# First block of a two-block transformer on one core: weights-moving products 512 wide, the residual's affine on VectorE, and the gated mix's affine taken through the token mix

## The chip, the cores and the metric

The kernel runs on one core of a Trainium2 chip. The metric is the device time of one execution in microseconds, and it is the median of three executions where a table says so. The engines are TensorE (PE, with its weight loads shown apart as PEld), VectorE (DVE), ScalarE (ACT), GpSimd (POOL) and SyncE (SP), which issues the DMA transfers.

## The reference

There are 256 tokens of 1024 features. The first block has two layers; layer 0 mixes with an RWKV-7 part and a differential attention (`ab_w_in`, `ab_w_out`), layer 1 with a gated token mix (`c_w_in`, `c_w_out`). The second block, not touched by the change, takes the result.

```python
for i in range(DEPTH):                       # DEPTH = 2
    if i % 2 == 0:
        p = x @ ab_w_in[j]
        mix = concatenate([rwkv7_mix(p[..., :1792]), diff_attention(p[..., 1792:])]) @ ab_w_out[j]
    else:
        mix = chunked_spatial_gating(x, ...) @ c_w_out[j]
    x = layer_norm(DEEPNORM_ALPHA * x + mix, ln1_g[i], ln1_b[i])
    x = layer_norm(DEEPNORM_ALPHA * x + conv_ffn(x, ...), ln2_g[i], ln2_b[i])

def chunked_spatial_gating(x, w_in, b_in, ln_g, ln_b, w_s, b_s):
    u, v = split(gelu(x @ w_in + b_in), 2)                   # 1024 features each
    v = layer_norm(v, ln_g, ln_b)
    vc = v.reshape(B, S // 128, 128, 8, 128)                 # chunks of 128 tokens, 8 groups of features
    ws = w_s * tril(ones)
    mixed = einsum('gts,bcsgd->bctgd', ws, vc) + b_s.T
    return u * mixed

def conv_ffn(x, w_up, conv_w, conv_b, w_down):               # 2816 wide
    gate, val = split(x @ w_up, 2)
    return (silu(causal_conv3(gate) + conv_b) * val) @ w_down
```

## The kernel before

Every float32 weight and activation is split exactly into a high and a low part, and each product is three matmuls: high by high, high by low, low by high. `wload` fetches 128 x 1024 weights (512 KB) into `wraw` on SP's queue, ACT casts the high part `whi`, DVE subtracts to get `wlo`. There are four buffers each of `wraw`, `whi` and `wlo`, and two extra for the first weights behind a norm (`hw`).

Two forms of product exist. In `w_stat` the weights are stationary and the 256 tokens move; its result has features on partitions. In `w_mov` 128 tokens of the activations are stationary and 256 columns of weights move; its result has tokens on partitions, and the column blocks of one weight tile cover both token tiles. `nat_gemm` (the attention's q, k, v and the gate's v), `nat_out` (the output products of both mixes) and the down product inside `conv_ffn` use `w_mov`. A PSUM bank holds 512 float32 for a partition, so a bank has a column block of both token tiles. PSUM pools: `pmm` 3 banks, `pss` 2, `pst` 2, `psf` 1. `z_add` adds a finished block into the residual `z`, which has tokens on partitions (two tiles t of 128 x 1024).

`layer_norm` then runs on `z`: four `bn_stats` over 256 columns for each t, `bn_aggr`, a power on POOL for the reciprocal root (`rs`), the normalisation on DVE in two halves, eight PE transposes for each t, and for each of eight feature chunks k the gain and bias on the way out of PSUM (`xf`, `xh`, on DVE or ACT), and `xl` = `xf` - `xh` on DVE. Last it puts the gain and the bias (`lrow`) also on `z` itself, for the next residual, with four 128 x 1024 operations on POOL that are pinned in program order:

```python
pin(self.pool.tensor_tensor(v, v, rows[:, 0], ALU.mult))
pin(self.pool.tensor_tensor(v, v, rows[:, 1], ALU.add))
```

The products that come next take chunk after chunk (`w_stat_k`, three column chunks, 72 matmuls), as `xh` and `xl` arrive; between them stand steps of the second block's modulation (`fillers`, written `sf<-wraw,cs`).

`gmlp` is the gated mix: three of the u chunks in that head, then v in four column blocks, v's norm on DVE with its gain and bias on DVE for t = 0 and POOL for t = 1, meanwhile u chunks 3 to 7, and at the end the token mix: for each of 8 groups and 2 token tiles a float32 matmul of `v` by the masked `wst`, and a one-row matmul that adds the bias `bs`. A list scheduler orders the instructions of each engine by its own estimates; only pinned ones stay as written.

## Time and profile before

| what | value |
|---|---|
| time, median of 3 | 2304.64 us (2303.82 to 2312.74) |
| span of the profiled execution | 2304.2 us, mean granted clock 0.986 |
| PE busy | 2230.4 us (97%) |
| DVE / ACT / POOL busy | 1354.0 / 931.6 / 294.7 us |
| first block, about | the first 800 us |

The span goes from the first to the last instruction. The granted clock is TensorE's, 1.00 for 2.4 GHz and 0.50 for 1.2 GHz. Instructions are pipelined, so a duration overlaps the next start; a pace is the distance between starts.

### The profile page before, as it was taken

The page shows a single profiled execution, that of the slowest core. Times are in us where ns is not written, and L with a number is a line of the kernel's source. Part 1 is how long each engine was busy: PE and PEld are TensorE (multiplying, and loading weights), DVE is VectorE, ACT ScalarE, POOL GpSimd, SP SyncE. Part 2 cuts the span into 40 slices and gives each one's busy share as a digit, 9 for nine tenths or more (in the row PEclk, how much of TensorE's full clock was granted, in tenths as well). Part 3 has the DMA queues.
Part 4 walks back from the last instruction along what each step waited for, and adds up shares of the span by engine and source line. Part 5 has one row for each costly group of instructions (what it writes and reads, how often), then busy time and mean ns, then how long its engine had stood idle before and what let it go on. Part 6 is the DMA issues. An engine that isn't in the chain of part 4 may idle for free. (4 is left out here: it accounts for less than half of the span.)

```text
span 2304.2 us, 37682 instructions
## 1 busy us (share of the span) xinstructions
PE 2230.4 (97%) x15048; PEld 1936.7 (84%) x15048; DVE 1354.0 (59%) x2361; ACT 931.6 (40%) x1589; POOL 294.7 (13%) x382
## 2 busy tenths in 40 slices
PE   8999899989999999999999999999999999999999
PEld 7867799978899988657778888888889878888999
DVE  6523777674867734665566446444345566766665
ACT  5322454442445433442333334233244443345443
POOL 1153200022100002001222000000000205420000
PEclk9999999997999999999999999999999999999999
DMA  7456666573665522123442242333333233245663
GB/s 237 135 170 212 201 206 185 171 242 95 222 188 168 174 74 83 51 85 105 150 136 74 87 119 73 92 101 92 101 111 93 74 95 94 90 133 165 183 183 128
DMA packets 90640, 310.06 MB, mean 135 GB/s; under 512 B 10257, under 2 KB 12433, under 8 KB 89826
## 3 DMA queue, kind: packets, MB, share of 16 engines
q1 hardware_dynamic: 90242, 307.30, 43.1%
q8 instruction: 118, 1.93, 0.3%
q14 instruction: 56, 0.46, 0.1%
q0 software_dynamic: 224, 0.36, 0.0%
HBM read 306.58 MB, written 1.05 MB: 134 GB/s over the span
## 5 line engine op out<-in xcount | busy, mean ns | idle before, releaser
L242 DVE TENSOR_TENSOR wlo<-wraw,whi 128x1024 fp32r<-128x1024 f32 x462 | 558.0, 1211 | 391.4 <-ACT whi L321 390.4
L321 ACT CAST whi<-wraw 128x1024 fp32r<-128x1024 f32 x494 | 492.8, 1001 | 726.2 <-PE mm L276 624.4
L276 PE MATMUL mm<-hh,whi 128*128 128x256 f32 (+1 forms) x1200 | 412.9, 346 | 4.3 <-ACT hh L254 2.4
L276 PE MATMUL mm<-hh,wlo 128*128 128x256 f32 (+1 forms) x1200 | 406.3, 339 | 0.0
L276 PE MATMUL mm<-hl,whi 128*128 128x256 f32 (+1 forms) x1200 | 405.4, 338 | 0.0
L276 PE MATMUL mm<-xh,whi 128*128 128x256 f32 x880 | 252.7, 288 | 8.2 <-ACT xh L321 7.3
L276 PE MATMUL mm<-xl,whi 128*128 128x256 f32 x880 | 253.8, 288 | 3.8 <-DVE xl L242 3.7
L276 PEld LDWEIGHTS mm<-hh,whi 128*128 128x128 f32 x1200 | 227.2, 190 | 32.4 <-issue 7.9
L276 PEld LDWEIGHTS mm<-hh,wlo 128*128 128x128 f32 x1200 | 227.7, 190 | 28.8 <-issue 3.6
L276 PE MATMUL mm<-xh,wlo 128*128 128x256 f32 x880 | 251.9, 286 | 0.0
L276 PEld LDWEIGHTS mm<-hl,whi 128*128 128x128 f32 x1200 | 228.0, 190 | 25.4 <-issue 3.1
L276 PE MATMUL mm<-whi,hh 128*128 128x256 f32 x736 | 205.9, 280 | 3.2 <-ACT vn L1326 2.4
L276 PE MATMUL mm<-whi,hl 128*128 128x256 f32 x736 | 205.6, 279 | 0.0
L276 PE MATMUL mm<-wlo,hh 128*128 128x256 f32 x736 | 205.5, 279 | 0.0
L276 PEld LDWEIGHTS mm<-xh,whi 128*128 128x128 f32 x880 | 171.5, 195 | 10.8 <-ACT xh L321 7.6
L276 PEld LDWEIGHTS mm<-xl,whi 128*128 128x128 f32 x880 | 171.8, 195 | 8.7 <-DVE xl L242 6.8
L276 PE MATMUL mm<-ul,whi 128*128 128x256 f32 (+1 forms) x536 | 176.7, 330 | 0.1
L276 PE MATMUL mm<-uh,wlo 128*128 128x256 f32 (+1 forms) x536 | 176.3, 329 | 0.0
L276 PE MATMUL mm<-uh,whi 128*128 128x256 f32 (+1 forms) x536 | 176.2, 330 | 0.0
L276 PEld LDWEIGHTS mm<-xh,wlo 128*128 128x128 f32 x880 | 171.8, 195 | 0.0
L276 PEld LDWEIGHTS mm<-whi,hh 128*128 128x128 f32 x736 | 140.0, 190 | 4.2 <-ACT vn L1326 2.8
L276 PEld LDWEIGHTS mm<-whi,hl 128*128 128x128 f32 x736 | 138.2, 188 | 0.8 <-issue 0.8
(411 smaller groups left out, 3959.8 us busy)
## 6 DMA issues: line engine op xcount, KB each, us to landing
wraw<-in_w_ff SPq DMA_DIRECT2D x128, 512.0 KB, 3.7
wraw<-in_w_mod SPq DMA_DIRECT2D x96, 512.0 KB, 4.2
wraw<-in_w_up SPq DMA_DIRECT2D x88, 512.0 KB, 3.7
wraw<-in_w_gate SPq DMA_DIRECT2D x48, 512.0 KB, 3.6
wraw<-in_w_dn SPq DMA_DIRECT2D x32, 512.0 KB, 3.6
wraw<-in_w_br SPq DMA_DIRECT2D x48, 256.0 KB, 2.6
wraw<-in_w_h SPq DMA_DIRECT2D x24, 512.0 KB, 3.7
wraw<-in_w_out SPq DMA_DIRECT2D x16, 512.0 KB, 3.8
```

Of the source, the lines that this page charges most:

```text
L242: (eng or self.dve).tensor_tensor(out, a, b, ALU.subtract)
L276: self.pe.matmul(out, lhsT, rhs, start=start, stop=stop, **k)
L321: self.act.copy(hi, src)
```

## The change

1. `w_wide` moves 512 columns of weights over one token tile, so a weight tile is 2 feature chunks by 512 columns instead of 4 by 256, and a column block takes two PSUM banks, one for each t. The attention's q, k, v, both `nat_out`, the gate's v and both down products use it. In the last group of the down product, and in the late half of `nat_out`, the last column block is ordered by t.
2. `bn_stats` covers 512 columns, `z_add` one t and 512 columns.
3. The residual's gain and bias go to DVE, not pinned, written later (`do_later`).
4. In `gmlp` the gain and the bias of v's norm are no longer applied to v. The bias goes through the mix once: two matmuls of `ones` by the masked `wst` give its column sums, and eight operations make `bs` from them; the gain is a per-feature column at the way out of PSUM. The one-row bias matmuls are gone, the mask product of `wst` goes from POOL to DVE, and the mix of two groups is written behind each u chunk from 4 on. `rows3` has 1024 columns less.

```diff
+def _pack_c(w):
+    k, n = w.shape
+    return np.ascontiguousarray(
+        w.reshape(k // 256, 2, 128, n // 512, 512).transpose(3, 0, 2, 1, 4)
+    ).reshape(n // 512 * (k // 256), 128, 1024)
...
+    def w_wide(self, out, hi, lo, xh, xl, k0, t, first, last):
+
+        for k in range(2):
+            wh, wl = hi[:, k * 512:(k + 1) * 512], lo[:, k * 512:(k + 1) * 512]
+            a, b = (x[:, k0 + k, t * 128:(t + 1) * 128] for x in (xh, xl))
+            self.mm(out, a, wh, start=first and k == 0, stop=False)
+            self.mm(out, a, wl, start=False, stop=False)
+            self.mm(out, b, wh, start=False, stop=last and k == 1)
+
+    def wide_gemm(self, w, cb, xh, xl):
+
+        banks = [self.pmm(), self.pmm()]
+        for kk in range(4):
+            hi, lo = self.wload(w[cb * 4 + kk])
+            for t in range(2):
+                self.w_wide(banks[t], hi, lo, xh, xl, 2 * kk, t, kk == 0, kk == 3)
+        return banks
...
-        load = lambda cb, h: self.wload(w[cb * 2 + h])
-        banks = [self.pmm() for _ in range(3)]
-        outs = lambda b: [b[:, 0:256], b[:, 256:512]]
-        last = [self.pss(), self.pss()]
-        halves = lambda h: [(*load(3, h), 4, 4 * h)]
-        for cb in range(3):
-            self.w_mov(outs(banks[cb]), *load(cb, early), yh, yl, 4, 256, (0, 1), True, False, k0=4 * early)
-        self.last_block(z, yh, yl, halves(early), ALPHA, last, True, False)
-        tiles = [load(cb, 1 - early) for cb in range(3)]
+
+
+        banks = [[self.pmm(), self.pmm()], [self.pmm(), self.pss()]]
+        for cb in range(2):
+            for i in range(2):
+                kk = 2 * early + i
+                hi, lo = self.wload(w[cb * 4 + kk])
+                for t in range(2):
+                    self.w_wide(banks[cb][t], hi, lo, yh, yl, 2 * kk, t, i == 0, False)
+        kks = [2 - 2 * early + i for i in range(2)]
+        tiles = [[self.wload(w[cb * 4 + kk]) for kk in kks] for cb in range(2)]
         for t in range(2):
-            for cb in range(3):
-                self.w_mov([outs(banks[cb])[t]], *tiles[cb], yh, yl, 4, 256, (t,), False, t == 1, k0=4 - 4 * early)
-                if t:
-                    self.z_add(z, cb, banks[cb], ALPHA)
-        self.last_block(z, yh, yl, halves(1 - early), ALPHA, last, False, True)
-
-    def z_add(self, z, cb, ps, scale):
-        zs = z.rearrange("p (t c) -> p t c", t=2)[:, :, cb * 256:(cb + 1) * 256]
-        self.stt(zs, zs, scale, ps.rearrange("p (t c) -> p t c", t=2), ALU.mult, ALU.add)
-
-    def last_block(self, z, yh, yl, tiles, scale=1.0, banks=None, first=True, last=True):
-        """Last column block of z = scale * z + y @ w, a bank for each token tile."""
-        banks = banks or [self.pmm(), self.pmm()]
-        for i, (hi, lo, nk, k0) in enumerate(tiles):
-            for t in range(2):
-                self.w_mov([banks[t][:, 0:256]], hi, lo, yh, yl, nk, 256, (t,), first and i == 0,
-                           last and i == len(tiles) - 1, k0=k0)
-        for t in range(2 if last else 0):
-            zs = z[:, t * D + 768:t * D + 1024]
-            self.stt(zs, zs, scale, banks[t][:, 0:256], ALU.mult, ALU.add)
+            for cb in range(2):
+                for kk, (hi, lo) in zip(kks, tiles[cb]):
+                    self.w_wide(banks[cb][t], hi, lo, yh, yl, 2 * kk, t, False, kk == kks[1])
+                self.z_add(z, cb, t, banks[cb][t], ALPHA)
+
+    def z_add(self, z, cb, t, ps, scale):
+        zs = z[:, t * D + cb * 512:t * D + cb * 512 + 512]
+        self.stt(zs, zs, scale, ps, ALU.mult, ALU.add)
...
-            pin = self.tc.keep_in_program_order
-            pin(self.pool.tensor_tensor(v, v, rows[:, 0], ALU.mult))
-            pin(self.pool.tensor_tensor(v, v, rows[:, 1], ALU.add))
+            self.later.append(lambda v=v: self.mul(v, v, rows[:, 0]))
+            self.later.append(lambda v=v: self.add(v, v, rows[:, 1]))
         return xh, xl
+
+    def do_later(self, n):
+        for _ in range(min(n, len(self.later))):
+            self.later.pop(0)()
...
+                    if cp:
+                        self.do_later(2)
...
-                def down(cb, k0, nk):
-                    if c0 < 16:
-                        src = A[f"w_dn{l}"][(c0 // 8) * 8 + cb * 2 + k0 // 4]
-                    else:
-                        src = A[f"w_dt{l}"][cb][:, k0 * 256:(k0 + nk) * 256]
-                    return (*self.wload(src, nk * 256), nk, k0)
-
-                parts = [(0, 4), (4, n - 4)]
-                for cb in range(4 if c0 < 16 else 3):
-                    ps = self.pmm()
-                    for i, (k0, nk) in enumerate(parts):
-                        hi, lo = down(cb, k0, nk)[:2]
-                        self.w_mov([ps[:, 0:256], ps[:, 256:512]], hi, lo, hh, hl, nk, 256, (0, 1), i == 0, i == 1, k0=k0)
-                    self.z_add(z, cb, ps, ALPHA if c0 == 0 else 1.0)
-                if c0 == 16:
-                    self.last_block(z, hh, hl, [down(3, *q) for q in parts])
+                for cb in range(2):
+                    banks = [self.pmm(), self.pmm()]
+                    nk = n // 2
+                    tiles = [self.wload(A[f"w_dn{l}"][c0 + cb * nk + kk]) for kk in range(nk)]
+                    order = [(t, kk) for kk in range(nk) for t in range(2)]
+                    if c0 == 16 and cb:
+                        order.sort()
+                    for t, kk in order:
+                        self.w_wide(banks[t], *tiles[kk], hh, hl, 2 * kk, t, kk == 0, kk == nk - 1)
+                        if kk == nk - 1:
+                            self.z_add(z, cb, t, banks[t], ALPHA if c0 == 0 else 1.0)
...
-            self.mul(wst, wst, triu.unsqueeze(1).to_broadcast([128, 8, 128]), self.pool)
-            bs = gp.tile([1, 8, 128], F32, name="bs")
-            nc.sync.dma_start(bs, A["b_s"].rearrange("p (g t) -> p g t", g=8))
             rows = gp.tile([128, NROWS3], F32, name="rows3")
             nc.sync.dma_start(rows, A["rows3"].partition_broadcast(128))
-            bv, lg, lb = rows[:, :1024], rows[:, 1024:2048], rows[:, 2048:]
+            bv, bs = rows[:, :1024], rows[:, 1024:].rearrange("p (g t) -> p g t", g=8)
...
-            for cb in range(4):
-                (ps,) = self.nat_gemm(A["w_c_v"], cb, xh, xl, (0, 1))
-                for k in range(0 if cb else 3):
-                    gelu_u(banks[k // 2], k)
-                sl = slice(cb * 256, cb * 256 + 256)
-                self.add(v[:, :, sl], ps, bv[:, sl].unsqueeze(1).to_broadcast([128, 2, 256]))
-                self.fn(v[:, :, sl], v[:, :, sl], AF.Gelu)
             st = rp.tile([128, 2, 2, 6], F32, name="st")
             mv = rp.tile([128, 2, 2], F32, name="mv")
             rs = rp.tile([128, 2], F32, name="rs")
+            for cb in range(2):
+                ps = self.wide_gemm(A["w_c_v"], cb, xh, xl)
+                for k in range(0 if cb else 3):
+                    gelu_u(banks[k // 2], k)
+                sl = slice(cb * 512, cb * 512 + 512)
+                for t in range(2):
+                    self.add(v[:, t, sl], ps[t], bv[:, sl])
+                    self.fn(v[:, t, sl], v[:, t, sl], AF.Gelu)
+                    self.dve.bn_stats(st[:, t, cb], v[:, t, sl])
+                if cb == 0:
+                    self.mul(wst, wst, triu.unsqueeze(1).to_broadcast([128, 8, 128]))
+                    for i in range(2):
+                        ps = self.pst()
+                        self.mm(ps, self.ones, wst[:, 4 * i:4 * i + 4].rearrange("p g t -> p (g t)"))
+                        for g in range(4 * i, 4 * i + 4):
+                            self.stt(bs[:, g], ps[:, g % 4 * 128:g % 4 * 128 + 128], self.col("c_ln_b", g), bs[:, g],
+                                     ALU.mult, ALU.add)
             for t in range(2):
-                for h in range(2):
-                    self.dve.bn_stats(st[:, t, h], v[:, t, h * 512:(h + 1) * 512])
                 self.dve.bn_aggr(mv[:, t], st[:, t])
             self.rsqrt(rs, mv[:, :, 1], 1e-5)
             for t in range(2):
                 self.ts(v[:, t], v[:, t], mv[:, t, 0:1], rs[:, t:t + 1], ALU.subtract, ALU.mult)
-                eng = self.pool if t else self.dve
-                self.mul(v[:, t], v[:, t], lg, eng)
-                self.add(v[:, t], v[:, t], lb, eng)
+            yh = yp.tile([128, KC, S], F32R, name="yh")
+            yl = yp.tile([128, KC, S], F32R, name="yl")
+
+            def mix(kp):
+                ps = self.pst()
+                m = tp.tile([128, 2, 2, 128], F32, name="m")
+                for j in range(2):
+                    g = 2 * kp + j
+                    for t in range(2):
+                        self.mm(ps[:, j * 256 + t * 128:j * 256 + t * 128 + 128], v[:, t, g * 128:(g + 1) * 128], wst[:, g])
+                    self.stt(m[:, j], ps[:, j * 256:j * 256 + 256].rearrange("p (t c) -> p t c", t=2),
+                             self.col("c_ln_g", g), bs[:, g].unsqueeze(1).to_broadcast([128, 2, 128]), ALU.mult, ALU.add)
+                sl = slice(2 * kp, 2 * kp + 2)
+                mf = m.rearrange("p j t c -> p j (t c)")
+                self.mul(mf, mf, uT[:, sl])
+                self.split(yh[:, sl], yl[:, sl], mf)
+
             for k in range(3, KC):
                 if k % 2 == 0 or k == 3:
                     ps = self.pmm()
                 self.w_stat(half(ps, k), *self.wload(A["w_c_u"][k]), xh, xl, KC)
-                if k % 2:
-                    for i in (k - 1, k):
-                        if i > 2:
-                            gelu_u(ps, i)
-            yh = self.fx.tile([128, KC, S], F32R, name="xh")
-            yl = self.fx.tile([128, KC, S], F32R, name="xl")
-            for kp in range(4):
-                ps = self.pst()
-                for j in range(2):
-                    g = 2 * kp + j
-                    for t in range(2):
-                        o = ps[:, j * 256 + t * 128:j * 256 + t * 128 + 128]
-                        self.mm(o, v[:, t, g * 128:(g + 1) * 128], wst[:, g], start=True, stop=False)
-                        self.mm(o, self.ones[0:1, :], bs[:, g], start=False, stop=True)
-                sl = slice(2 * kp, 2 * kp + 2)
-                self.mul(uT[:, sl], uT[:, sl], ps.rearrange("p (j t) -> p j t", j=2))
-                self.split(yh[:, sl], yl[:, sl], uT[:, sl])
+                gelu_u(ps, k)
+                if k == 3:
+                    self.do_later(4)
+                if k >= 4:
+                    mix(k - 4)
...
-            for cb in range(2):
-                (ps,) = self.nat_gemm(A["w_diff"], 2 * i + cb, xh, xl, (0, 1))
-                self.act.mul(n[:, :, cb * 256:(cb + 1) * 256], ps, 0.125 if i == 0 else 1.0)
-                if cb == 0:
-                    yield
+            for t, ps in enumerate(self.wide_gemm(A["w_diff"], i, xh, xl)):
+                self.act.mul(n[:, t], ps, 0.125 if i == 0 else 1.0)
```

The rows of DVE at the first norm behind `nat_out` (layer 0), before (`z` residual, `lrow` its gain and bias, `xf`, `xh`, `xl` the chunks that the next products take):

```order
L248 TENSOR_SCALAR z_101<-z_101,mv0_2938,rs0_2939 128x512 x2
L246 TENSOR_SCALAR rs1_2959<-mv1_2958 128x1
L248 TENSOR_SCALAR z_101<-z_101,mv1_2958,rs1_2959 128x512 x2
L248 TENSOR_SCALAR xf_2979<-st_2933,cols_79 128x256
L248 TENSOR_SCALAR xf_2987<-st_2934,cols_79 128x256
L242 TENSOR_TENSOR xl_2978<-xf_2979,xh_2977 128x256
L242 TENSOR_TENSOR xl_2978<-xf_2983,xh_2977 128x256
```

The same place after the change:

```order
L252 TENSOR_SCALAR rs1_2715<-mv1_2714 128x1
L242 TENSOR_TENSOR z_101<-z_101,lrow_2537 128x1024
L254 TENSOR_SCALAR z_101<-z_101,mv1_2714,rs1_2715 128x512 x2
L254 TENSOR_SCALAR xf_2733<-st_2691,cols_79 128x256
L245 TENSOR_TENSOR z_101<-z_101,lrow_2537 128x1024
L248 TENSOR_TENSOR xl_2732<-xf_2733,xh_2731 128x256
L254 TENSOR_SCALAR xf_2741<-st_2692,cols_79 128x256
L248 TENSOR_TENSOR xl_2732<-xf_2737,xh_2731 128x256
L242 TENSOR_TENSOR z_101<-z_101,lrow_2537 128x1024
L248 TENSOR_TENSOR xl_2732<-xf_2741,xh_2731 128x256
```

Although it is written later, the scheduler has put the gain of t = 0 ahead of the normalisation of t = 1, and the rest of the affine between the `xl`.

At the second norm (in front of `gmlp`) DVE has, after the change, also the mask product of `wst` and the assembly of the bias `rows3`:

```order
L245 TENSOR_TENSOR z_101<-z_101,lrow_4060 128x1024
L252 TENSOR_SCALAR rs1_4772<-mv1_4771 128x1
L242 TENSOR_TENSOR wst_4834<-wst_4834,triu_4836 128x1024
L254 TENSOR_SCALAR z_101<-z_101,mv1_4771,rs1_4772 128x512 x2
L254 TENSOR_SCALAR xf_4790<-st_4748,cols_79 128x256
L242 TENSOR_TENSOR z_101<-z_101,lrow_4060 128x1024
L248 TENSOR_TENSOR xl_4789<-xf_4790,xh_4788 128x256
L248 TENSOR_TENSOR xl_4789<-xf_4794,xh_4788 128x256
L254 TENSOR_SCALAR xf_4798<-st_4749,cols_79 128x256
L257 SCALAR_TENSOR_TENSOR rows3_4838<-st_5037,cols_79,rows3_4838 128x128 x3
L248 TENSOR_TENSOR wlo_4958<-wraw_4955,whi_4957 128x1024
```

The mask product now stands ahead of the normalisation of t = 1, and the subtraction of a weight tile between the `xl`.

On PE the token mix before is one piece behind the last u chunk:

```order
L276 MATMUL mm<-xh,wlo 128x256
L276 MATMUL st<-wst,v 128x128
L276 MATMUL st<-bs,ones 128x128
L276 MATMUL st<-wst,v 128x128
L276 MATMUL st<-bs,ones 128x128
```

After the change it starts among the products of the u chunks:

```order
L282 MATMUL mm<-xh,whi 128x256
L282 MATMUL st<-wst,v 128x128 x2
L282 MATMUL mm<-xl,whi 128x256
L282 MATMUL mm<-xh,wlo 128x256
L282 MATMUL mm<-xh,whi 128x256
L282 MATMUL st<-wst,v 128x128 x2
L282 MATMUL mm<-xl,whi 128x256
```

The sixteen matmuls of the mix are spread over some 80 rows, the first of them 49 rows of the u chunks behind the last product of v; the sixteen of the bias are gone.

## Rows read from the trace of the kernel before

**Rows 1.** Page: busy time, share of the span and instructions of each engine.

```profile
PE 2230.4 (97%) x15048; PEld 1936.7 (84%) x15048; DVE 1354.0 (59%) x2361; ACT 931.6 (40%) x1589; POOL 294.7 (13%) x382
```

**Rows 2.** Waits of PE from 0 to 650: total us, times, longest.

```profile
PE mm L276 <- ACT xh L321: 7.3, 2, 6.9
...
PE mm L276 <- DVE xl L242: 5.1, 6, 1.4
...
PE st L276 <- POOL v L239: 2.4, 1, 2.4
```

**Rows 3.** Windows: stretch, length, busy (count) by engine, granted clock, DMA.

```profile
277.20:335.20 58.00, 53.85 (x427) 49.42 (x426) 48.46 (x73) 28.12 (x39) 11.52 (x10) 0.97 0.67 210
...
538.50:563.30 24.80, 22.36 (x66) 15.34 (x64) 8.10 (x8) 3.64 (x6) 3.15 (x1) 0.57 0.17 52
```

**Rows 4.** Windows of two spells at the lower clock, same columns.

```profile
541.80:569.10 27.30, 27.30 (x87) 20.57 (x88) 6.36 (x9) 2.72 (x5) 0.14 (x2) 0.50 0.09 27
596.40:606.70 10.30, 10.04 (x45) 8.15 (x46) 8.79 (x12) 6.86 (x15) 6.32 (x3) 0.50 0.47 154
```

**Rows 5.** Timeline of PE, down product, 256 wide: start us, us, instruction.

```profile
339.75 0.28 PE L276 MATMUL mm<-whi,hh 128*128 128x256 f32 x1
...
354.95 0.28 PE L276 MATMUL mm<-whi,hh 128*128 128x256 f32 x1
```

**Rows 6.** Timeline of PE, second output product, 256 wide.

```profile
569.20 0.28 PE L276 MATMUL mm<-whi,xh 128*128 128x256 f32 x1
...
588.88 0.28 PE L276 MATMUL ss<-whi,xl 128*128 128x256 f32 x1
```

**Rows 7.** Timeline of PE, second block, 512 wide.

```profile
1459.62 0.39 PE L276 MATMUL mm<-ul,whi 128*128 128x512 f32 x1
...
1499.92 0.39 PE L276 MATMUL mm<-hl,whi 128*128 128x512 f32 x1
```

**Rows 8.** Timeline of DVE in the first and the second norm.

```profile
278.99 1.00 DVE L248 TENSOR_SCALAR z<-z,mv,rs 128x512 f32<-128x512 f32 x2 [0.42 <-POOL rs L285]
...
280.72 3.03 DVE L248 TENSOR_SCALAR z<-z,mv,rs 128x512 f32<-128x512 f32 x2 [0.67 <-POOL rs L285]
283.68 0.99 DVE L248 TENSOR_SCALAR xf<-st,cols 128x256 f32<-128x256 f32 x2
284.84 3.93 DVE L242 TENSOR_TENSOR xl<-xf,xh 128x256 fp32r<-128x256 f32 x2 [0.18 <-ACT xh L254]
...
296.15 0.42 DVE L242 TENSOR_TENSOR xl<-xf,xh 128x256 fp32r<-128x256 f32 x1
...
481.89 5.18 DVE L248 TENSOR_SCALAR z<-z,mv,rs 128x512 f32<-128x512 f32 x2 [0.67 <-POOL rs L285]
```

**Rows 9.** Timeline of POOL in the first norm.

```profile
280.83 2.64 POOL L499 TENSOR_TENSOR z<-z,lrow 128x1024 f32<-128x1024 f32 x1
```

**Rows 10.** DMA issues between 470 and 500: count, KB each, us to landing.

```profile
wst<-in_w_s SPq DMA_DIRECT2D x1, 512.0 KB, 5.4
```

**Rows 11.** Groups on PE between 538.5 and 563.3.

```profile
L276 PE MATMUL st<-bs,ones 1*128 1x128 f32 x32 | 12.4, 486 | 0.0
```

**Rows 12.** Timeline of PE at the start of the token mix.

```profile
538.47 0.38 PE L276 MATMUL st<-wst,v 128*128 128x128 f32 x2
538.78 0.48 PE L276 MATMUL st<-bs,ones 1*128 1x128 f32 x2
541.71 0.71 PE L276 MATMUL st<-wst,v 128*128 128x128 f32 x2 [2.44 <-POOL v L239]
```

**Rows 13.** Page, groups: busy us, mean ns, idle before; and DMA issues.

```profile
L242 DVE TENSOR_TENSOR wlo<-wraw,whi 128x1024 fp32r<-128x1024 f32 x462 | 558.0, 1211 | 391.4 <-ACT whi L321 390.4
L321 ACT CAST whi<-wraw 128x1024 fp32r<-128x1024 f32 x494 | 492.8, 1001 | 726.2 <-PE mm L276 624.4
...
wraw<-in_w_dn SPq DMA_DIRECT2D x32, 512.0 KB, 3.6
```

**Rows 14.** Tile `z`, its adds: ns min/median/max, first and last start.

```profile
L251 DVE SCALAR_TENSOR_TENSOR z<-z,mm x32: 404/682/689, 271.6 to 797.9; 128x512 f32<-128x512 f32 x28, 128x256 f32<-128x256 f32 x4
```

More of the change, by code (lines that the diff above doesn't have):

```diff
@@ L145, in _pack @@
     o["w_rwkv"] = _pack_b(w[:, :1792])
-    o["w_diff"] = _pack_a(w[:, 1792:])
+    o["w_diff"] = _pack_c(w[:, 1792:])
     o["w_lora"] = np.concatenate([i["ab_w2"][0], i["ab_a2"][0]], 0)
     o["w_g2"] = i["ab_g2"][0]
-    o["w_ab_out"] = _pack_a(i["ab_w_out"][0])
+    o["w_ab_out"] = _pack_c(i["ab_w_out"][0])
     o["w_c_u"] = _pack_b(i["c_w_in"][0][:, :D])
-    o["w_c_v"] = _pack_a(i["c_w_in"][0][:, D:])
-    o["w_c_out"] = _pack_a(i["c_w_out"][0])
+    o["w_c_v"] = _pack_c(i["c_w_in"][0][:, D:])
+    o["w_c_out"] = _pack_c(i["c_w_out"][0])
     o["w_s"] = np.ascontiguousarray(i["c_w_s"][0].transpose(2, 0, 1)).reshape(128, 1024)
-    o["b_s"] = i["c_b_s"][0].reshape(1, 1024)
     for l in (0, 1):
@@ L217, in __init__ @@
         self.upto, self.dbg = upto, dbg or {}
+        self.later = []
         nc = self.nc
@@ L401, in first_block @@
             xh, xl = self.layer_norm(z, "ln2", 0, rows)
-            yh, yl = self.gmlp(xh, xl)
-            rows = self.norm_rows(2)
-            self.nat_out(A["w_c_out"], yh, yl, z, 0)
+            with tc.tile_pool(name="gy", bufs=1) as yp:
+                yh, yl = self.gmlp(yp, xh, xl)
+                rows = self.norm_rows(2)
+                self.nat_out(A["w_c_out"], yh, yl, z, 0)
             xh, xl = self.layer_norm(z, "ln1", 1, rows)
@@ L461, in layer_norm @@
         for t in range(2):
-            st = lp.tile([128, 4, 6], F32, name=f"st{t}")
+            st = lp.tile([128, 2, 6], F32, name=f"st{t}")
             mv = lp.tile([128, 2], F32, name=f"mv{t}")
             rs = lp.tile([128, 1], F32, name=f"rs{t}")
-            for g in range(4):
+            for g in range(2):
                 self.dve.bn_stats(st[:, g], zv[:, t, g])
@@ L994, in diff_proj @@
             yield
-        for cb in range(2):
-            (ps,) = self.nat_gemm(A["w_diff"], 4 + cb, xh, xl, (0, 1))
-            self.act.copy(vd[:, :, cb * 256:(cb + 1) * 256], ps)
-            yield
+        for t, ps in enumerate(self.wide_gemm(A["w_diff"], 2, xh, xl)):
+            self.act.copy(vd[:, t], ps)
+        yield
     def diff_attn(self, es, qT, kT, vd, row):
```

18 lines of the change are left out of this document (9 added, 9 removed).

## Prediction

> **What bounds the kernel now.** I read the page first. PE is busy for 97% of the span, DVE for 59%, POOL for 13% [rows 1], so time can come out in two ways only: PE's work gets shorter, or one of the few places where PE waits or runs at half clock gets shorter. Then the waits of PE in the first block [rows 2]: they are small, and they stand in the norms (a first `xh`, then the `xl` on DVE) and at the token mix (2.4 us for `v` on POOL). Not in this list is any wait of a product for `whi` or `wlo`, so weights arrive in time today. Third, windows by stage: the stretch behind the first `nat_out` loses about 4 us to gaps (53.85 busy in 58.00), and the token mix takes 24.8 us for 16 + 16 small matmuls at a mean clock of 0.57 [rows 3]. Last, the spells at 1.2 GHz: one goes from 541.8 to 569.1, that is from the first gap of the mix to some way into the output products, another covers 10.3 us of the third norm [rows 4]. So the change is priced in three parts: the pace of the products, the norms, and the mix.
>
> **Part 1, wide products.** Counted from the diff: down products 2 x (192 + 192 + 144) = 1056 matmuls of 256 columns become 528 of 512; two `nat_out` (2 x 192), v (192) and q, k, v of the attention (288), together 864, become 432. The price of a narrow one is a pace: in the down product 130 starts from 339.75 to 354.95, 129 steps, 15.20 / 129 = 117.8 ns [rows 5]; in the output product 165 starts from 569.20 to 588.88, 19.68 / 164 = 120.0 ns [rows 6]. I use the second for v and the attention too, which is an extension. A 512-wide product with weights moving does not exist in this trace. The nearest is one with 512 columns of activations moving over the same 128 x 128: 178 starts from 1459.62 to 1499.92, 40.30 / 177 = 227.7 ns [rows 7]. With it the down products give 528 x (235.6 - 227.7) = 4.2 us and the others 432 x (240.0 - 227.7) = 5.3 us, together **9.5 us**. Bounds: 0, if a wide one costs just two narrow ones, and 11.4, if it were 2 ns quicker than that row (960 x 2 ns more). I take the row, because operands, sizes and number of columns agree and only the roles differ.
>
> A rule speaks against this part. The row shows two narrow products at 240.0 ns against 227.7 for one wide one [rows 6, 7], so each start costs about 12 ns beyond its columns. The Trainium skill, TensorE: Matmul & The Clock Gate, section Back-to-back issue gap, gives for an isolated product at full clock N/2.4 + 2.5 ns, so 2.5 ns is all that joining two would save; worked out from that page it is an estimate of 960 x 2.5 ns = 2.4 us in place of the 9.5. The trace has 117.8 and 120.0 ns where the formula has 109.2, so it does not agree for the narrow ones, and I stay with the rows. The same section gives 131 ns as a sustained spacing at 512 columns, by which the gain would be an estimate of 100 us; the 227.7 ns measured [rows 7] do not bear that out, so it gets no chance.
>
> What could make the wide form wait: a column block now holds two PSUM banks of `pmm`'s three. The next block's first product takes the third bank; its second bank is that of t = 0 of the block before, whose `z_add` may start six wide products before that block's end, and six more products of the next block lie ahead: 12 x 0.228 = 2.7 us of cover for a 0.68 us add [rows 14] behind at most one 1.21 us subtraction [rows 13]. I cost it at nothing; without that cover it would be up to 1.9 us for a block.
>
> **Part 2, the norms.** In the first norm T0, the end of the output products, is 277.2. The normalisation of t = 0 takes 1.00 us for its two halves, that of t = 1 takes 3.03, and two `xl` take 3.93 where one alone takes 0.42 [rows 8]. What differs is POOL: its 2.64 us product on `z` runs from 280.83, beside the slow ones [rows 9]. In the second norm the same normalisation takes 5.18. The last `xl` ends at 296.57, T0 + 19.4. After the change POOL has no such work, but the order shows the affine back inside the same chain on DVE: one 128 x 1024 operation ahead of the normalisation of t = 1 and, up to the last `xl`, two more, with three subtractions `wlo`. Worked out: before, t = 1 starts at T0 + 3.5, 0.67 of it a wait for `rs` [rows 8]. The gain of t = 0 (1.21, as a `wlo` of that size [rows 13]) fills that wait and costs 0.5 beyond it, and the statistics of t = 0, done earlier now, give about as much back: T0 + 3.5 again. Then 1.0 for the normalisation, four `xf` at 0.5, eight `xl` at 0.42, and five operations of 1.21: 1.0 + 2.0 + 3.4 + 6.1 = 12.5, so the last `xl` ends at T0 + 16.0. That is 3.4 us less; I take **3.0**, for gaps between ACT and DVE that do not vanish. PE needs some 9 products behind it in either case.
>
> Second norm: `wst` lands 5.4 us behind its issue [rows 10], which itself comes only behind the last down product, and its mask product now stands in DVE's queue ahead of the normalisation of t = 1. So that one ends at about T0 + 0.4 + 5.4 + 1.2 + 1.0 = 8.0; before it was 481.89 + 5.18 = 487.07 [rows 8] with T0 = 478.0, the end of the last down product, so 9.1. Behind the waiting mask product stand all of xf and xl, and PE for them. The `xl` then run without POOL, but with one more affine operation, the assembly of the bias and three `wlo`. I take **2.0** of the possible 4. The two matmuls of ones fall into PE's gaps there. Third norm: as the first, **3.0**; it has a spell of 10.3 us at half clock [rows 4], which I leave as it is. Last norm, with no affine: **0.7**, from statistics of t = 0 that are done ahead of the end. Sum **8.7**. Bounds: 0, if the four affine operations of each of three norms (12 x 1.21 = 14.5) eat what POOL's absence gives (3 x about 5); 14, if also the half-clock spells go.
>
> **Part 3, the mix.** The stage from 538.5 to 563.3 is 24.8 us [rows 3], and the one-row matmuls are half of its PE time [rows 11]. After the change 16 matmuls stay and stand among products. At full clock the first of them, of two records, takes 538.78 - 538.47 = 0.31 us [rows 12], so 16 x 0.31 = 5.0. The affine of v on POOL, for which PE waits 2.4 us today [rows 2, 12], is gone; from the last product of v to the first mix there are 49 products of 0.12 = 5.9 us of cover, and the chain (add, gelu, statistics, root on POOL, two normalisations) is nearer to 7, so I put 1.0 us of wait. 24.8 - 5.0 - 1.0 = 18.8. The half-clock spell, if PE stays dense, does not come: of it 563.3 to 569.1 lies in the output products, where 5.8 us at half the clock [rows 4] do the work of 2.9 at best; I take 2.5 as given back. Together **21.3**. Bounds: 16, if the clock falls anyway and the wait is 3 us more; 23.7, if there is no wait and matmuls take 0.22.
>
> **Sum.** 9.5 + 8.7 + 21.3 = 39.5 us. The profiled span is 2304.2, the median of three runs 2304.64, so the profiled execution may stand for the median: 2304.2 - 39.5 = 2264.7, **2265 us**.
>
> **The rivals.**
> - *Wide costs two narrow.* For it: the trace has no wide product with weights moving. Then part 1 gives 0 to 2.4 and the time is 2272 to 2274. Against: the shape of the row used is the same [rows 7].
> - *The affine eats the norms.* For it: the order, which has put back on DVE's chain what was to be deferred; against: what POOL's neighbourhood costs now. Norms give 0: 2273; with a late `wst` or late weight tiles, 2277.
> - *The mix stays slow.* If DVE's products, splits and subtractions between u chunks hold PE and the clock falls again, 6 to 10 us of part 3 come back: 2271 to 2275, or 2280 together with one of the above.
> - *More than forecast.* The half-clock spells of the norms go too, and the mix matmuls cost 0.22: 2253, and with a shorter last norm 2250.
> - *The other side: weight tiles come in too late.* A column block now goes through three or four tiles of 512 KB, all written ahead of its first product, where a narrow block had two. A buffer is refilled by a transfer of 3.6, a cast of 1.00 and a subtraction of 1.21 [rows 13], 5.8 us, in part behind other DVE work. 21 blocks (12 down, 4 output, 2 v, 3 attention) that each wait once for the whole would add 122 us: 2387. It decides at 39.5 / 21 = 1.9 us for each block (no gain left), and slower by more than 0.5% from (39.5 + 11.5) / 21 = 2.4. Against it: the late half of `nat_out` already holds four tiles, and no product waits for `whi` or `wlo`; bytes per column of work are the same.
>
> **How the numbers follow.** A measurement of this kernel can tell about 0.5%, 11.5 us, from no change. Chances: forecast 0.54 (2257 to 2271), wide costs two narrow 0.12, affine 0.13, mix 0.07, more 0.09, other side 0.05. Faster by over 0.5% means under 2293: all but the last and a small part of combined rivals, 0.91; within 0.5% 0.05; slower 0.04. The range goes from the edge of *more* (2249) past the affine and mix rivals (2283): **2249 to 2283**, with about 0.08 above and 0.05 below.
>
> **What would show it.** Part 1: down products at a pace of 228 ns, not 236 or 240, and no gap at a block's start. Part 2: normalisation of t = 1 at 1.0 us, two `xl` at 0.84, the last `xl` at T0 + 16 in the first norm; in the second, a wait of DVE's mask product on the transfer of `wst`. Part 3: no stretch of mix matmuls alone, clock 1.00 at the start of the second output product, and 0 to 2 us of wait for `v`. I am wrong if products wait for `wlo` at each block, if `xl` in the norms stand behind `wlo` that wait for ACT, or if the interleaved mix runs at 0.50.

## The result, and the profile after

The changed kernel takes 2271.05 us (median of four runs, 2265.48 to 2272.87), the one before 2304.3 us on the same chip: a ratio of 0.984, 95% interval [0.982, 0.986], so 32 to 41 us less. That is 1.6% faster, as forecast, and inside the range; the forecast of 2265 was 6 us too low. The profiled execution is the shortest of the four: its span is 2263.4 us, 40.8 below that of before.

The page of the changed kernel, busy time of each engine, against [rows 1]:

```profile
PE 2200.2 (97%) x14060; PEld 1877.9 (83%) x14060; DVE 1345.0 (59%) x2364; ACT 929.9 (41%) x1585; POOL 254.7 (11%) x367
```

PE is busy for 30 us less, in part because its clock is higher; the other 11 of the 41 us are waits that went. Windows of the changed kernel (stretch, length, busy and count of PE, PEld, DVE, ACT, POOL, granted clock, DMA share, GB/s): layer-0 output product, first norm with the up products, second norm to the last u product ahead of the mix, the mix, second output product, third norm:

```profile
248.75:277.72 28.97, 26.33 (x104) 20.68 (x105) 19.48 (x27) 10.10 (x18) 4.25 (x7) 0.88 0.56 184
277.72:333.00 55.28, 52.56 (x425) 48.28 (x424) 45.77 (x74) 28.19 (x39) 1.90 (x5) 1.00 0.69 229
473.55:514.50 40.95, 37.92 (x205) 30.45 (x204) 30.76 (x47) 20.21 (x29) 0.55 (x1) 0.96 0.71 245
514.50:534.30 19.80, 18.96 (x156) 18.39 (x155) 16.43 (x26) 9.68 (x15) 1.76 (x2) 1.00 0.44 145
534.30:555.50 21.20, 21.20 (x96) 17.50 (x95) 16.14 (x22) 8.86 (x10) 0.68 (x3) 1.00 0.56 191
555.50:611.20 55.70, 53.40 (x433) 49.18 (x432) 48.32 (x92) 31.13 (x46) 1.87 (x5) 1.00 0.74 240
```

The reader is to see three things. The first norm's stretch is 55.3 us where it was 58.0 [rows 3]. The mix no longer has a stretch of its own, and the second output product runs at 1.00 from its start, 21.2 us. But the layer-0 output product got longer and has a clock of 0.88. The same stretch in the kernel before:

```profile
250.60:277.20 26.60, 24.64 (x199) 23.94 (x199) 19.27 (x28) 10.04 (x18) 3.69 (x6) 1.00 0.65 218
```

PE's timeline of the changed kernel there, and a window of the granted clock:

```profile
253.28 0.63 PE L286 MATMUL st<-ident,o 128*128 128x128 f32 x4 [1.52 <-DVE o L242]
254.58 0.80 PE L282 MATMUL mm<-whi,xh 128*128 128x512 f32 x1 [0.68 <-ACT xh L989]
...
258.54 1.05 PE L286 MATMUL st<-ident,y 128*128 128x128 f32 x4
```

```profile
254.60:260.60 6.00, 5.56 (x14) 4.04 (x15) 2.93 (x5) 0.97 (x2) 0.53 (x3) 0.50 0.32 109
```

Only 12 wide products stand ahead of `o` (30 narrow ones did before). PE waits 1.52 us for `o`, then for the `xh` made of it, and then goes on at 0.50 for 6 us; the transposes of `y` stand behind these slow products.

The down products (the first of these rows to the last are 78 steps of PE's timeline, 17.68 / 78 = 226.7 ns):

```profile
335.11 0.39 PE L282 MATMUL mm<-whi,hh 128*128 128x512 f32 x1
...
352.79 0.39 PE L282 MATMUL mm<-whi,hh 128*128 128x512 f32 x1
```

DVE's timeline in the first norm, against [rows 8], and the first of the second:

```profile
280.01 1.23 DVE L242 TENSOR_TENSOR z<-z,lrow 128x1024 f32<-128x1024 f32 x1
281.68 1.00 DVE L254 TENSOR_SCALAR z<-z,mv,rs 128x512 f32<-128x512 f32 x2 [0.44 <-POOL rs L291]
...
283.22 1.21 DVE L245 TENSOR_TENSOR z<-z,lrow 128x1024 f32<-128x1024 f32 x1
284.35 0.42 DVE L248 TENSOR_TENSOR xl<-xf,xh 128x256 fp32r<-128x256 f32 x1
...
285.48 1.22 DVE L242 TENSOR_TENSOR z<-z,lrow 128x1024 f32<-128x1024 f32 x1
...
293.44 0.75 DVE L248 TENSOR_TENSOR xl<-xf,xh 128x256 fp32r<-128x256 f32 x2
...
475.12 1.21 DVE L242 TENSOR_TENSOR z<-z,lrow 128x1024 f32<-128x1024 f32 x1
...
476.37 1.23 DVE L245 TENSOR_TENSOR z<-z,lrow 128x1024 f32<-128x1024 f32 x1
...
477.75 1.25 DVE L242 TENSOR_TENSOR wst<-wst,triu 128x1024 f32<-128x1024 f32 x1
478.92 0.99 DVE L254 TENSOR_SCALAR z<-z,mv,rs 128x512 f32<-128x512 f32 x2
```

The normalisation of t = 1 takes 1.00 where it took 3.03 and 5.18, the last two `xl` of the first norm end at 294.2. T0, the end of the output products, is 277.7 here, so that is T0 + 16.5 (before T0 + 19.4, forecast T0 + 16.0). Three affine operations stand ahead of them. In the second norm the mask product of `wst` starts without a wait, behind two affine operations and ahead of the normalisation of t = 1. PE waits 3.03 us for that normalisation, and from 479.7 to 483.1 its clock is 0.50:

```profile
479.51 1.00 PE L286 MATMUL st<-ident,z 128*128 128x128 f32 x4 [3.03 <-DVE z L254]
```

To compare kernels I cut the first block on PE's timeline at the first and last layer-0 output product, the first and last down product of layer 0, the last second output product, the first down product of layer 1 and the last transpose of `z`. Each number is the difference of two starts, us, one profiled execution each. (Where the first output product is narrow, a single product of it runs 2.5 us ahead of the rest; it is left out.)

| kernel | output 0 | norm 1, up | rest of ffn 0 | norm 2, gate, output 1 | norm 3, up | rest of ffn 1 | sum |
|---|---|---|---|---|---|---|---|
| before | 26.5 | 58.1 | 142.7 | 111.0 | 60.5 | 154.8 | 553.6 |
| changed | 28.7 | 55.5 | 140.3 | 81.9 | 56.0 | 152.9 | 515.3 |
| again | 28.8 | 55.3 | 140.3 | 82.4 | 59.3 | 152.9 | 519.0 |
| wide_only | 29.2 | 58.7 | 140.3 | 111.4 | 60.9 | 152.9 | 553.4 |
| narrow | 26.5 | 53.8 | 142.7 | 83.4 | 54.2 | 154.8 | 515.4 |
| affine_pool | 28.7 | 59.9 | 140.3 | 87.3 | 60.9 | 152.9 | 530.0 |
| affine_late | 28.3 | 53.8 | 140.3 | 79.2 | 54.9 | 152.9 | 509.4 |
| nat0_narrow | 26.5 | 54.8 | 140.3 | 82.2 | 60.9 | 152.9 | 517.6 |
| mix_end | 29.0 | 55.0 | 140.3 | 83.3 | 57.9 | 152.9 | 518.4 |
| bias_rows | 28.7 | 55.5 | 140.3 | 93.2 | 55.2 | 152.9 | 525.8 |
| late_nat0 | 26.5 | 53.5 | 140.3 | 79.8 | 54.4 | 152.9 | 507.4 |
| narrow_late | 26.5 | 53.3 | 142.7 | 82.2 | 56.3 | 154.8 | 515.8 |

What lies ahead (248.7 to 254.9 us) and behind (the second block, 1494 to 1504 us) varies by several us among these kernels without order; the first is 248.8 and 250.1 in two executions of the changed kernel itself.

### The profile page after: what moved, and what is told of

Read it like the earlier page. It is cut to its first block, busy times and chain, and to the rows that moved or that the text cites. A ratio compares the mean times of both kernels' runs of the same rounds, so it can differ in the third digit from the quotient of the medians.

```text
span 2263.4 us, 35673 instructions
## 1 busy us (share of the span) xinstructions
PE 2200.2 (97%) x14060; PEld 1877.9 (83%) x14060; DVE 1345.0 (59%) x2364; ACT 929.9 (41%) x1585; POOL 254.7 (11%) x367
## 5 line engine op out<-in xcount | busy, mean ns | idle before, releaser
L327 ACT CAST whi<-wraw 128x1024 fp32r<-128x1024 f32 (+1 forms) x490 | 492.7, 1008 | 722.8 <-PE mm L282 620.0
L282 PE MATMUL mm<-whi,hh 128*128 128x256 f32 (+1 forms) x560 | 177.7, 318 | 2.0 <-ACT vn L1346 1.2
L282 PEld LDWEIGHTS mm<-xh,whi 128*128 128x128 f32 x880 | 169.0, 193 | 10.8 <-ACT xh L327 7.9
L282 PE MATMUL mm<-wlo,hh 128*128 128x256 f32 (+1 forms) x560 | 177.4, 317 | 0.0
L282 PE MATMUL mm<-whi,hl 128*128 128x256 f32 (+1 forms) x560 | 177.4, 317 | 0.0
L257 DVE SCALAR_TENSOR_TENSOR X<-mm,mod,X 128x256 f32<-128x256 f32 x96 | 43.8, 481 | 121.4 <-PE mm L282 121.4
L282 PEld LDWEIGHTS mm<-whi,hh 128*128 128x128 f32 x560 | 106.7, 191 | 10.0 <-ACT vn L1346 1.6
```

The costliest lines, as they stand in the source:

```text
L257: self.dve.scalar_tensor_tensor(out, a, s, b, op0, op1)
L282: self.pe.matmul(out, lhsT, rhs, start=start, stop=stop, **k)
L327: self.act.copy(hi, src)
```

## The experiments

My theory: three parts that add up (wide products, POOL out of the norms, the mix), less a loss in the layer-0 output product. The main rival: what looks like one part comes from another.

**Each part alone.** `wide_only` is the kernel before with the first two items of the change; `narrow` is the changed kernel with `nat_gemm`, the old `nat_out`, the old down product and the norms' statistics over 256 columns back.

> The kernel before with the wide products alone (and the statistics and adds that go with them); affine on POOL and token mix as before. Theory (products cheaper by 8 to 13 ns a pair, of which some 2 us are given back in the first output product, where PE waits for o at the lower clock): 9.5 - 2 = 7.5 us less than before, some 2297, down products at a pace of 227 ns, the norms' slow xl (3.9 us for two) still there. Rival (a wide product costs two narrow ones, and what the change gave came from elsewhere): 2302 to 2304.

Ratio 0.996 [0.995, 0.998], 2297.8 us: as expected by the time. By the trace not: the table has 553.4 against 553.6. The down products give 2.4 and 1.9, the output product takes back 2.7, the heads of two norms 0.6 and 0.4 and the stage with the gate 0.4, and 5.5 us of this execution's shorter span lie in the second block. So what the products alone are worth is not settled by this run.

> The changed kernel with its narrow products back (256 wide, one bank for both token tiles); affine on VectorE and the new token mix stay. Theory (the three parts add up): norms and mix give 2304 - 9 - 22 = some 2273 to 2276, and the first output product has no slow stretch. Rival (wide blocks with one token tile ahead are what makes the norms short): 2280 or more.

Ratio 0.983 [0.981, 0.985], 2268.2 us. Norms and mix alone give what the whole change gives (0.984). In the table 515.4 against 515.3: wide products gain 2.4, 1.5 and 1.9 and lose 2.2, 1.7 and 1.8. Neither case of the expectation: the parts add up, but the wide products' part is about zero here. The two kernels differ in one more thing, though: the scheduler places the affine elsewhere. In the first norm of `narrow` two affine operations stand ahead of the last `xl`, both behind the normalisation of t = 1, where the changed kernel has three:

```profile
286.56 1.22 DVE L237 TENSOR_TENSOR z<-z,lrow 128x1024 f32<-128x1024 f32 x1
...
288.82 1.22 DVE L240 TENSOR_TENSOR z<-z,lrow 128x1024 f32<-128x1024 f32 x1
...
296.16 0.75 DVE L243 TENSOR_TENSOR xl<-xf,xh 128x256 fp32r<-128x256 f32 x2
```

So this run does not price the products alone; `narrow_late`, below, has the affine out of the way.

**The affine.**

```diff
-            self.later.append(lambda v=v: self.mul(v, v, rows[:, 0]))     # affine_pool
+            pin(self.pool.tensor_tensor(v, v, rows[:, 0], ALU.mult))
-            self.later.append(lambda v=v: self.mul(v, v, rows[:, 0]))     # affine_late
+            self.later.append(lambda v=v: pin(self.dve.tensor_tensor(v, v, rows[:, 0], ALU.mult)))
```

(The gain only; the bias likewise. `affine_late` also spreads the four in `gmlp`, one behind each mix step.)

> The changed kernel with the residual's gain and bias back on POOL, pinned. Theory (POOL beside DVE is what made the xl and the second normalisation slow): the xl take 3.9 us for two again, the heads of three norms end 2.5 to 4.5 us later, 2277 to 2283. Rival (the norms became shorter because the statistics of the first token tile are ready earlier, and DVE pays for the affine what POOL's absence gives): 2270 to 2273.

Ratio 0.990 [0.988, 0.992], 2282.9 us, 12 more than the changed kernel on its chip (13 by the ratios): the theory. Timelines of DVE and of POOL in its first norm:

```profile
282.46 5.04 DVE L254 TENSOR_SCALAR z<-z,mv,rs 128x512 f32<-128x512 f32 x2 [0.66 <-POOL rs L291]
...
289.47 2.04 DVE L248 TENSOR_TENSOR xl<-xf,xh 128x256 fp32r<-128x256 f32 x1 [0.47 <-ACT xh L506]
```

```profile
282.39 2.34 POOL L513 TENSOR_TENSOR z<-z,lrow 128x1024 f32<-128x1024 f32 x1
...
288.75 2.48 POOL L513 TENSOR_TENSOR z<-z,lrow 128x1024 f32<-128x1024 f32 x1 [1.54 <-PE ss L286]
```

What takes 1.00 and 0.42 alone takes 5.04 and 2.04 beside POOL. In the table the three norms are 4.4, 5.4 and 4.9 us longer. A part of that is the clock: PE waits up to 2.5 us at a time for `z`, and the mean is 0.94 in the first and the third of these stretches, where the changed kernel has 1.00. The Trainium skill, SBUF — State Buffer, section Who interferes with whom, says that a VectorE instruction with two SBUF inputs contends with a GpSimd instruction that reads SBUF; the `xl` here agrees, its 2.04 us end just behind POOL's 2.48.

> The changed kernel with the affine still on VectorE, but pinned where it is written: behind the second pair of column chunks of the feed-forward, and one operation behind each mix step. Theory (DVE's chain sets the head behind a norm, three or four operations of 1.2 us stand in it): 1.5 to 3 us less in each of three norms, 2262 to 2267. Rival (PE's transposes, ACT's casts and the fillers set the head, the affine sits in DVE's gaps): 2270 to 2272. Third: the affine now holds a subtraction that products wait for: above 2273.

Ratio 0.981 [0.979, 0.982], 2262.4 us: the theory. The stages of the three norms lose 1.7, 2.7 and 1.1 us against the changed kernel; the last is less than the 1.5 expected, and in the second PE waits 0.4 us for `z` instead of 3.03 and the spell at 0.50 behind it does not come (clock 1.00 in the whole stage). DVE's timeline in the first norm has no `lrow` left:

```profile
285.78 1.00 DVE L254 TENSOR_SCALAR z<-z,mv,rs 128x512 f32<-128x512 f32 x2 [0.66 <-POOL rs L291]
286.86 0.99 DVE L254 TENSOR_SCALAR xf<-st,cols 128x256 f32<-128x256 f32 x2
```

**A base for the next, and the spread.**

> The changed kernel once more, on the chip of the three that follow, as their base and for a second trace. Theory (its spread of some 7 us is in the spells of the lower clock behind the norms and in the first output product): 2265 to 2273, with the first output product at 28.5 us again and spells that come and go elsewhere.

`again` is the copy that the next runs are compared with: 2270.1 us, ratio 0.983 [0.981, 0.985]. Its third norm is 59.3 where the first trace has 56.0, and the window shows why:

```profile
564.00:574.00 10.00, 8.61 (x46) 7.78 (x47) 6.67 (x13) 5.27 (x12) 0.00 (x0) 0.66 0.58 199
556.90:616.20 59.30, 56.86 (x435) 52.46 (x434) 48.47 (x92) 31.24 (x46) 1.87 (x5) 0.94 0.72 226
```

The clock falls behind this norm in one execution and not in the other. The layer-0 output product is at 28.8 again.

**The layer-0 output product.** `nat0_narrow` packs `w_ab_out` as before and calls the old `nat_out` for it.

```diff
-            self.nat_out(A["w_ab_out"], yh, yl, z)
+            self.nat_out_n(A["w_ab_out"], yh, yl, z)
```

> The changed kernel with the layer-0 output product alone 256 wide again, as before. Theory (with blocks of two banks, only 12 wide products lie ahead of o, PE waits there, then runs at half clock, and the modulation's weights come late behind it): the output product takes 26.5 instead of 28.7 us and the first norm is up to 1.7 us shorter, 2 to 4 us less than the unchanged copy beside it. Rival (the wait for o is set by the chain of the mix, whatever the products are): the same time within 1 us.

2267.5 us, ratio 0.982 [0.980, 0.984]; 2.6 us below the copy, with intervals that overlap. The trace has the theory's place: 26.5 us as before, the norm behind it 0.5 shorter.

**The mix.** `mix_end` writes `for kp in range(4): mix(kp)` behind the loop of the u chunks; `bias_rows` adds a one-row matmul to each of the sixteen.

```diff
+                        self.mm(o, self.ones[0:1, :], zr, start=False, stop=True)
```

> The changed kernel with the token mix written behind all u chunks instead of between them; its bias is still taken through the mix. Theory (most of the 24.8 us stage was the clock and one-row matmuls, so what counts is that PE stays dense): the mix of 16 matmuls alone, 5 us at full clock, plus a tail on DVE that the next products wait for, 2 to 6 us more than the copy. Rival A (interleaving is what saved the stage): 10 us or more, with a spell at half clock that reaches into the output product. Rival B (dropping the one-row matmuls alone did it): no more than 1 us.

2270.7 us, ratio 0.983 [0.981, 0.985], no different from the copy; the stage is 0.9 us longer. PE's timeline:

```profile
528.73 1.06 PE L282 MATMUL st<-wst,v 128*128 128x128 f32 x8
530.17 0.49 PE L282 MATMUL st<-wst,v 128*128 128x128 f32 x2 [0.38 <-DVE m L257]
...
533.37 2.12 PE L282 MATMUL st<-wst,v 128*128 128x128 f32 x14
536.03 0.50 PE L282 MATMUL mm<-whi,yh 128*128 128x512 f32 x1 [0.54 <-ACT yh L327]
```

Sixteen matmuls of two records each need no cover; what waits remain are below 0.6 us. My theory asked for 2 to 6; rival B was right.

> The changed kernel with sixteen one-row matmuls of zeros added in the mix, where the kernel before had those of the bias; the output is unchanged. Theory (a one-row matmul costs 0.2 to 0.3 us among dense products): 3.5 to 5 us more than the copy, no spell at half clock. Rival (in the stage before, the one-row matmuls brought the clock down): a stretch at 0.50 appears around the mix, 8 us or more.

2279.5 us, ratio 0.987 [0.985, 0.989]: 9.4 us more than the copy, 10.8 in the stage. Rows of PE, and those of the changed kernel without them:

```profile
525.33 0.48 PE L282 MATMUL st<-zr,ones 1*128 1x128 f32 x2
525.74 0.49 PE L282 MATMUL st<-wst,v 128*128 128x128 f32 x2
526.16 0.48 PE L282 MATMUL st<-zr,ones 1*128 1x128 f32 x2
```

```profile
521.38 0.68 PE L282 MATMUL st<-wst,v 128*128 128x128 f32 x4 [0.84 <-DVE v L254]
522.25 0.61 PE L282 MATMUL st<-wst,v 128*128 128x128 f32 x4
```

A pair takes 526.16 - 525.33 = 0.83 us. Without such pairs a matmul of the mix takes 0.22: the eight records of four matmuls in `mix_end` last 1.06 us, the last one 0.28 of it, so the other seven stand 0.11 apart, and two are a matmul. So a one-row matmul costs 0.61 us with what it does to its neighbour, 16 x 0.61 = 9.8. The rest is the clock: behind the first three pairs it falls to 0.50, which the changed kernel does not do in its mix.

```profile
527.30:530.70 3.40, 3.40 (x16) 3.05 (x15) 0.48 (x1) 0.00 (x0) 0.00 (x0) 0.50 0.50 154
```

Work that takes 3.4 us at half clock takes 1.7 or more at full clock, so at most 1.7 of the 10.8 are the spell, and the one-row matmuls are worth 9 to 10 at full clock. The theory was wrong on the price and on the spell; the rival came in a small form, 3.4 us instead of 8, in one execution.

**Both repairs, and what wide products are worth with them.**

> The changed kernel with both repairs that the runs so far point to: the affine pinned late on VectorE, and the layer-0 output product 256 wide. Theory (the two losses are separate: a chain on VectorE behind the norms, and PE's wait for o with the spell behind it): 2262.4 - 2.5 = some 2260, ratio to before some 0.979 to 0.980. Rival (one hides the other, or the spells of the clock eat it): no faster than the late affine alone, 0.9806.

2261.5 us, ratio 0.981 [0.979, 0.983]. By the time it is not to be told from `affine_late`, as the rival has it; by the table it is the shortest first block (507.4, 2.0 less). Windows (columns as above): first output product, first norm, gate, third norm, all at 1.00:

```profile
250.60:277.40 26.80, 24.80 (x203) 24.05 (x204) 19.08 (x24) 10.11 (x18) 3.69 (x6) 1.00 0.63 218
277.40:330.70 53.30, 51.42 (x426) 48.29 (x426) 46.40 (x77) 27.81 (x39) 1.50 (x6) 1.00 0.69 221
471.20:551.00 79.80, 77.73 (x453) 65.57 (x452) 63.23 (x93) 38.93 (x53) 3.25 (x6) 1.00 0.63 212
551.00:605.20 54.20, 53.45 (x434) 49.27 (x433) 47.35 (x90) 30.93 (x46) 0.95 (x5) 1.00 0.76 245
```

> All products narrow again, new token mix, affine pinned late. Theory (wide blocks give 4.3 us in the down products and 1.5 around the gate, and cost 2.2 in the first output product and up to 1.7 in each norm's head through late weights of the modulation): about as fast as the wide kernel with both repairs, 2259 to 2263. Rival (wide products are worth their 9.5 us once the affine is out of the way): 2267 or more.

2270.5 us, ratio 0.985 [0.983, 0.988]. On this chip 9.0 us more than the wide one, 8.4 in the table (2.4 + 1.9 in the down products, 2.4 in the stage with the gate, 1.9 in the third norm, 0.2 back in the first): the rival. The 1.9 of the third norm are not shown to be the products': `narrow` has 54.2 there, as short as the wide one's 54.4, while this execution has a spell at 0.50 and 1.7 us of waits for the modulation's weights.

```profile
561.50:564.90 3.40, 3.40 (x16) 2.85 (x15) 2.23 (x7) 0.60 (x2) 0.55 (x1) 0.50 0.71 281
```

That leaves 6.5, where part 1 had 4.2 + 1.2 + 1.2 = 6.6 for the down products, v and the second output product. That is closer than the working deserves: the second output product of `narrow_late` runs at 113 ns, where width gains nothing, so about 1.2 of the 2.4 in its stage has a cause that was not found. The theory, that wide products gain nothing, had counted up to 1.7 in each norm's head as theirs.

**What a narrow product costs.**

```diff
-            yh = self.fx.tile([128, KC, S], F32R, name="xh")      # y_own
+            yh = yp.tile([128, KC, S], F32R, name="yh")
-            self.fx = mk("fx", 1)                                 # swap
             fz = mk("fz", 1)
+            self.fx = mk("fx", 1)
```

> The kernel before with the gate's result, yh and yl, in a pool of its own, away from the place that the activations x have; nothing else. Theory (the price of a 256-wide product depends on where its operands lie in SBUF, and the new kernels with 113 ns there show that): 113 ns a product in the second output product, where the kernel before has 120. Rival (the 113 ns came from what else runs at that time, less work on DVE and POOL): 120 ns as before.

One run, 2305.2 us beside 2305.2 of before. PE in the second output product of `y_own`, 256 wide; 68 steps, 7.71 / 68 = 113.4 ns, where [rows 6] has 120.0:

```profile
581.88 0.28 PE L276 MATMUL mm<-whi,yh 128*128 128x256 f32 x1
...
589.59 0.28 PE L276 MATMUL mm<-whi,yl 128*128 128x256 f32 x1
```

> The changed kernel with the pools of the activations x and of z in the other order, so that xh and xl lie 11.5 KB further from the weights. If the distance from the weights sets the price of a 256-wide product, the up products go from 120 to some 118 ns or less; if it is another property of the place, 120 as before.

One run, 2267.9 us; the up products stay at 120 ns (384 of them in 46.07 us), so this shift changes nothing. But in the up products `xh` and `xl` move and the weights are stationary, and in `y_own` it was the stationary operand that got another place. So distance from the weights is excluded for the moving operand and this one shift only. That the place of the stationary operand matters is shown, by what rule is open.

## Why the prediction was right, point by point

- **Part 1, wide products (9.5 us).** The price was right, 226.7 ns for 227.7. The term for the down products was right, 4.2 forecast and 2.4 + 1.9 measured. Of the other 5.3 only 1.5 show against `narrow`, at the gate. The step that failed is "I cost it at nothing": I had looked for a wait in PSUM banks, but in the layer-0 output product PE waits for `o` with less work ahead of it, and the lower clock follows; 2.2 us more, where 96 x 12.3 ns = 1.2 less were forecast. All eight traces in which this product is wide have a spell at 0.50 in it (mean clock of the stretch 0.88, in `affine_late` 0.94); the six in which it is narrow have 1.00. What the heads of the norms lose against `narrow` is not the products': with the affine pinned the first stretch is 53.5 wide and 53.3 narrow. Fillers that wait for their weights are not theirs either. Waits of PE in the changed kernel, first 640 us, where before had 1.6 us of this kind in the same part:

```profile
PE sf L282 <- DMA wraw<-in_w_mod: 3.8, 4, 1.7
```

  Between 270 and 620 us `narrow_late` has 3.9 of them with narrow products, `late_nat0` 0.3 with wide ones. One gain was luck: the changed kernel also gives `yh` and `yl` a pool of their own, and there a narrow product takes 113.4 ns (`y_own`), so the 1.2 us of the second output product would have come with the pool alone. The formula of the Trainium skill, TensorE: Matmul & The Clock Gate, section Back-to-back issue gap, gives 109.2 ns for 256 columns, an estimate; `y_own` has 113.4, so part of the 12 ns of overhead that I read off the rows is the place of the operands. Its 2.5 ns for a start still do not explain the 117.8 of the down product, whose gain was measured.
- **Part 2, the norms (8.7 us).** Right mechanism. The first norm gave 2.6 of 3.0; the third 4.5 in one execution and 1.2 in another, by the clock. The second was mis-sized: putting the affine back on POOL costs it 5.4 us where I had taken 2.0. Up to 1.7 of that is the clock (6.8 us at 0.50 in `affine_pool`, from 484.7, 3.4 in the changed kernel). For the rest, I had expected DVE to wait for `wst`. It landed sooner, and DVE had two affine operations to do in the meantime; in the changed kernel's list of DMA issues (count, KB, us to landing) against [rows 10]:

```profile
wst<-in_w_s SPq DMA_DIRECT2D x1, 512.0 KB, 3.7
```

  That the affine stands in DVE's chain and costs there was read from the order, and `affine_late` shows the size: 1.7 + 2.7 + 1.1. One reading was wrong, with no term on it: the longest wait for a first `xh` in [rows 2], 6.9 us, lies in the first 30 us of the kernel and not in a norm, and the norms' own largest wait of PE, 5.5 us for `z`, is not among those rows.
- **Part 3, the mix (21.3 us).** For norm 2, gate and output product together I had 2.0 + 21.3 + 1.2 + 1.2 = 25.7; the stage gave 29.1. Of that the affine on POOL is 5.4. The working inside was wrong: a matmul of the mix costs 0.22 us, not the 0.31 of [rows 12], which is the distance to a one-row matmul; the one-row matmuls are worth 9 to 10 at full clock; the interleaving is worth 0.9 in the stage and nothing by the time. The wait for `v` is 0.84 us, 1.0 forecast. That the lower clock would go with the stage, and give back the start of the output product, was right.
- **The sum.** 39.5 was forecast and 40.8 is the difference of the two spans, in part by luck: the first output product gave 3.4 less than forecast, the stage with the gate 3.4 more. The 1.8 of q, k and v lie ahead of the table, where starts differ by 6 us, and no run shows them. The median lies 6 us above the forecast. The times lie some 2 us above the spans, and a span was put for a time. The rest is that the profiled execution was the shortest: the span of `again` is 5.2 us longer, 3.3 of them in the third norm, by the clock, and 1.4 ahead of the first output product. On the chip of `again` the medians are 39.0 us apart, so 6 us are no more than chips and executions differ by.
- **Rivals.** Of "the other side", weights too late, nothing came that belongs to the wide form: no product of the changed kernel waits for `whi` or `wlo` in the first 640 us, and the waits for the modulation's weights come and go with either form. "Wide costs two narrow" is false for the price, except in the second output product. "The affine eats the norms" came in part, the 1.7 + 2.7 + 1.1 that pinning gives back. "More than forecast" came in part too: the spells at 0.50 of the first and the third norm are gone in the profiled execution.

Open: the worth of the wide products alone. It is 8.8 us by the time of `wide_only` and nothing by its trace of the first block, with the affine on POOL; with both losses repaired it is 9.0 us by the time and 6.5 by the table without the spell.

## What to carry to other kernels

An operation that is written later is not later if a scheduler may hoist it; read the order, and pin it. When two small products become one large one, look at what stood between them: work that covered a wait is now coarser, and a wait of 1.5 us can be followed by 6 us at half clock. Before a small matmul is called cheap by its columns, time it beside its neighbours: a one-row matmul between large ones cost 0.61 us here, nearly three times the 0.22 of a whole one. Two kernels that differ in one form of product can differ in the scheduler's order too; pin the rest before the form is priced.

## What was not expected of the hardware

A 256-wide product went from 120.0 to 113.4 ns when only its stationary operand was put elsewhere in SBUF, with the same instruction and shape; two such cost 226.8, the same as one of 512. The clock fell to 0.50 in the layer-0 output product of all eight wide traces, in the changed kernel after 1.52 and 0.68 us of waits with little between them, and in none of the six narrow ones (in the kernel before PE waits 0.5 us for `o` there, and 1.4 for an `xl` further on). It also fell to 0.50 for 3.4 us when one-row matmuls of zeros were put into the mix, behind three of them.
